# Score products of full height and operand rows at one place modulo 256, in two chained transformer blocks on one core

## The chip, the core and the metric

The kernel runs on one core of a Trainium2 chip. The metric is the device time of one execution in microseconds; the times before are 2703.43, 2702.10 and 2704.92 us, median 2703.43 us. Names of engines: PE is TensorE (PEld its weight loads), DVE is VectorE, ACT is ScalarE, POOL is GpSimd, SP is the queue that issues most DMAs.

## The reference, cut to what matters

Two blocks of two layers each run one after the other on 256 tokens of width 1024. A layer is: half a SwiGLU feed-forward (FFN), a mixer, half an FFN. Block 1 carries a second stream of 256 context tokens; block 2 has one stream. The part that the change touches is the mixer of block 1:

```python
hx = modulate(rms_norm(x), mx[3], mx[4])
qx, kx, vx, upx, ufx = split_in(hx @ w_in[layer])
s = jnp.einsum('bqkgd,bskd->bkgqs', qb, k_all) * ATTN_SCALE      # 8 query heads, 2 key heads, width 64
p = jax.nn.softmax(s, axis=-1)
yp = jnp.einsum('blgc,gcd->blgd', pool_minus_self(u_pool), pool_w_l)   # 4 groups, 64 x 64 each
```

Latent queries attend to 512 keys (latent and context), context queries, in layer 0 alone, to 256.

## The kernel before, in words

**Split products.** Operands are float32 split in a high and a low part of type fp32r (`xhi`, `xlo` for activations, `whi`, `wlo` for weights, `h` for the inner FFN activations with both parts in one tile). `mm3` (lines 245 to 249) makes every large product from three matmuls into one PSUM tile: high by high (L247), low by high and high by low (L248, L249).

**FFN.** `prod` in `ffn` runs over 8 row tiles k of the model width; for each k it issues the three products with a 128x128 stationary weight tile and the activations `xhi[:, k]`, `xlo[:, k]` as the moving operand. In the profile these are `g<-xhi,whi`, `u<-xlo,whi` and so on, 24 products per tile of 128 inner columns and matrix. They are 512 columns wide where both streams run together and 258 wide with one stream (256 tokens and two more columns). The down product (`d<-h,whi`) moves `h`, 512 or 256 wide. Mixers use the same helper: `z` has the activations stationary and moves weights, `o` (output projection) and `fp` move the activations.

**Places in SBUF.** `xhi` and `xlo` are tiles [128, 8, 514] of 4-byte elements, so `xhi[:, k]` starts 2056 bytes behind `xhi[:, k-1]`. Weights lie in 4096-byte tiles, `h` and most mixer tensors in the 4096-byte slots of the pool `blk` (`BLK` = 17 of them, `slot`). In the built program the start bytes modulo 256 are: `xhi[:, k]` 128 + 8k, `xlo[:, k]` 192 + 8k, weights 0, `blk` slots 0.

**Mixer 1** (`mixer1`, once per layer of block 1). Keys are split in `use_kv`: `kk` holds per key head four planes of 64 (line 1173 on): high, high, low, and an unused one. `turn_k` transposes them to `khh` (high over high, 128 rows) and `klo` (low, 64 rows). Queries are transposed to 128 rows, high over low. `scores` makes a head's scores from two matmuls: L1205 on all 128 rows (query high and low by key high) and L1206 on the first 64 rows (query high by key low). `attend` (line 1011 on) is software-pipelined over heads: in step i PE makes the scores of head i (`s`), transposes the probabilities of head i-2 (`tp<-c_ident,prob`, L1004) and multiplies those of head i-3 by the values (`o<-v,PT`, L1041), while DVE takes the maximum and ACT the exponential. Steps of the pooling and Fourier mixers (`pool_fft`) fill in between. Layer 0 has 16 heads of 512 keys and 16 of 256, layer 1 16 of 512. `poolw` (line 1243) multiplies two pooled groups of 64 rows by their own 64x64 weights, two plain float32 matmuls on a quarter of the array each.

The order on each engine is that of the code; no scheduler moves instructions.

Of the kernel before, what the change touches and what calls it, by code (L numbers as in the profile page):

```python
# [11 lines left out]
F32R = mybir.dt.float32r  # L12
# [7 lines left out]
P = 128  # L20
D = 1024
KT = D // P
T = 256
# [5 lines left out]
WINDOWS = (2, 4, 8, 16)  # L29

WBUF = 5
BLK = 17
AHEAD, TAIL, TEND = (3, 4, 4, 4), 0, 3
WA = (range(8), range(0, 8, 2))
FSPLIT = {False: [(0, FT)], True: [(0, FT // 2), (FT // 2, FT)]}
# [9 lines left out]
def f32v(t):  # L45
    return t.bitcast(F32)


def kp(w):
    return w.rearrange("(kt p) n -> p kt n", p=P)  # L50


class Net:
# [5 lines left out]
    def __init__(self, tc, a, es):  # L59
# [4 lines left out]
        self.wsp = pool("wsp", WBUF)  # L64
        self.blk = pool("blk", BLK)
        self.adaw = pool("adaw", 2)
# [195 lines left out]
    def setup(self):  # L262
        nc, a = self.nc, self.a
        self.x = self.const.tile([P, KT, 512], F32, name="xstate")

        self.xh = self.const.tile([P, KT, 514], F32R, name="xhi")
        self.xl = self.const.tile([P, KT, 514], F32R, name="xlo")
        self.mods = {}
        self.pairs = {l: self.const.tile([P, 2, 72], F32, name=f"mod1{l}") for l in range(2)}
        for l in range(2):  # L270
            for v in range(2):
                self.mods["1", l, v] = self.pairs[l][:, v]
            self.mods["2", l, 2] = self.const.tile([P, 72], F32, name=f"mod2{l}")
        self.ones = self.const.tile([P, 2], F32, name="ones")
        nc.vector.memset(self.ones, 1.0)
        self.mhalf = self.const.tile([P, 16], F32, name="mhalf")
        nc.vector.memset(self.mhalf, -0.5)
        self.sc01 = self.const.tile([P, KT, 2], F32, name="csilu01")
        nc.sync.dma_start(self.sc01, a["ccols"])
        nc.scalar.activation(self.sc01, self.sc01, AF.Silu)  # L280
        self.cb = {}
        self.ident = self.cload("ident", [P, P])
        self.adab = {}
        for b in "12":
            for l in range(2):
                self.adab[b, l] = self.const.tile([P, 72], F32, name=f"adab{b}{l}")
        nc.gpsimd.dma_start(self.adab["1", 0], a["ada_b1"][0])
        self.load_stream(0)
        self.cb = {}
# [816 lines left out]
    def mixer1(self, l, nx):  # L1106
        nc, a = self.nc, self.a
# [9 lines left out]
        self.fetch(gains, a["qk_gain"][l, None].to_broadcast([P, 2, 2, 64]))  # L1117
        rot = gr[:, 8:].rearrange("p (t i a) d -> p t i a d", t=2, i=2)
        khh = self.slot([P, 2, 512], "khh", F32R)
        klo = self.slot([P, 2, 512], "klo", F32R)  # L1120
        v = self.slot([P, 4, P], "v")
        zz, kk, u, qT, rq = {}, {}, {}, {}, {}
        A, B = slice(0, 32), slice(32, 64)

        def gained(dst, src, st, t, i, n):

            bc = lambda w: w.unsqueeze(1).to_broadcast([P, n, w.shape[1]])
            if st:
                nc.vector.tensor_mul(dst, src, bc(gains[:, 0, i]))
                return  # L1130
            sw = self.w2("sw")[:, :n * 64].rearrange("p (h d) -> p h d", d=64)
            nc.vector.tensor_mul(sw[:, :, A], src[:, :, B], bc(rot[:, t, 1, i, A]))
            nc.vector.tensor_mul(sw[:, :, B], src[:, :, A], bc(rot[:, t, 1, i, B]))
            nc.vector.tensor_mul(dst, src, bc(rot[:, t, 0, i]))
            nc.vector.tensor_add(dst, dst, sw)

        def squares(src, n, name):
            sq = self.w2("qks")[:, :n * 64].rearrange("p (h d) -> p h d", d=64)
            nc.scalar.activation(sq, src, AF.Square)
            m = self.sml.tile([P, n], F32, name=name + "s", tag=name + "s", bufs=2)  # L1140
            nc.vector.reduce_sum(m, sq, axis=AX.X)
            return m
# [21 lines left out]
        def use_kv(st, pss):  # L1164
            for t in range(2):
                s = pss[t][:, :P].rearrange("p (h d) -> p h d", d=64)
                nc.scalar.copy(v[:, st * 2 + t], pss[t][:, P:])
                m = squares(s, 2, "k")
                rk = self.small(2)
                nc.vector.tensor_scalar(m, m, 1.0 / 64, EPS, op0=ALU.mult, op1=ALU.add)  # L1170
                nc.gpsimd.tensor_tensor(rk, m, self.mhalf[:, :2], op=ALU.pow)
                zk = self.w1("zk")[:, :P].rearrange("p (h d) -> p h d", d=64)
                gained(zk, s, st, t, 1, 2)
                nc.vector.tensor_mul(zk, zk, rk.unsqueeze(2).to_broadcast([P, 2, 64]))
                if t == 0:
                    kt = self.slot((P, 4, 4, 64), "kk", F32R)
                kk[st, t] = kt[:, 2 * t:2 * t + 2]
                nc.scalar.copy(kk[st, t][:, :, 0], zk)
                nc.scalar.copy(kk[st, t][:, :, 1], zk)
                nc.vector.tensor_sub(kk[st, t][:, :, 2], zk, f32v(kk[st, t][:, :, 0]))  # L1180

        def turn_k(st):
            for t in range(2):
                c = slice(st * T + t * P, st * T + (t + 1) * P)
                kf = f32v(kk[st, t])
                ps = self.transposes([kf[:, g, 0:2].rearrange("p a d -> p (a d)") for g in range(2)]
                                     + [kf[:, g, 2] for g in range(2)])
                nc.scalar.copy(khh[:, :, c], ps[:, :T].rearrange("p (g c) -> p g c", g=2))
                nc.scalar.copy(klo[:64, :, c], ps[:64, T:].rearrange("p (g c) -> p g c", g=2))

        def turn_q(st):
            qT[st] = [self.slot([P, 4, T], "qT", F32R) for _ in range(2)]
# [6 lines left out]
        def batches(st):  # L1199
            k0 = 0 if st == 0 else T  # L1200
            nk = 512 - k0

            def scores(s, h, qt, nk):
                q = qT[st][h // 4][:, h % 4, qt * P:(qt + 1) * P]
                nc.tensor.matmul(s, q, khh[:, h // 4, k0:], start=True, stop=False)  # L1205
                nc.tensor.matmul(s, q[:64], klo[:64, h // 4, k0:], start=False, stop=True)  # L1206

            return [dict(heads=range(8), qt=qt, nk=nk, hd=64, scores=scores, k0=0, col=st * T,
                         scale=lambda h, qt: rq[st, qt][:, h:h + 1],
                         v=lambda c, h: v[:, k0 // P + c, 64 * (h // 4):64 * (h // 4) + 64]) for qt in range(2)]  # L1210
# [3 lines left out]
        def pool_fft(st):  # L1214

            s = slice(st * T, (st + 1) * T)
            b = {}

            def load():
                if st == 0:  # L1220
                    pw = self.slot([P, 4, 256], "pw")
                    self.fetch(pw[:, 0, :P], a["pool_w"][l])
                    self.fetch(pw[:, 1:3], kp(a["fft_w"][l]))
                    self.fetch(pw[:, 3], a["chdft"].rearrange("p a b -> p (a b)"))
                    dft = self.slot([P, 2, 512], "dft")
                    self.fetch(dft, a["dft"])
                    mats.update(pw=pw, dft=dft)
                b.update(mats)
                for i in range(2):
                    b[i] = self.slot([P, 2, 2, T], "band")  # L1230
                    self.fetch(b[i], a["band"][i])
# [10 lines left out]

            def poolw(i):
                ps = self.smps("pl")
                for g in range(2):
                    hp = slice(64 * g, 64 * g + 64)
                    nc.tensor.matmul(ps[hp, :T], b["pw"][hp, 0, i * 64:i * 64 + 64], b["yp"][hp, i],
                                     start=True, stop=True)
                return lambda: self.split_ps(self.xh[:, 4 + i, s], self.xl[:, 4 + i, s], ps[:, :T],
                                             self.pscale[:, l * 2 + i:l * 2 + i + 1])  # L1250

# [37 lines left out]
        for t in range(2):  # L1289
            nc.vector.tensor_mul(rot[:, t], gains, rope1[:, t].unsqueeze(2).to_broadcast([P, 2, 2, 64]))  # L1290
        wk = self.tok_w(win[:, :, 512:768], 256)
        use_kv(0, self.tok_mm(0, wk, 256, free=False))
        psk = self.tok_mm(T, wk, 256)
        use_kv(1, psk)
# [440 lines left out]
def _tiles(w):  # L1735

    s = w.shape[:-2]
    k, m = w.shape[-2:]
    w = w.reshape(s + (k // P, P, m // P, P))
    n = len(s)  # L1740
    return np.ascontiguousarray(w.transpose(tuple(range(n)) + (n + 2, n + 1, n, n + 3)))


def _cols(v):

    return np.ascontiguousarray(np.asarray(v).reshape(-1, P).T)
# [42 lines left out]
def _layout(i):  # L1789
    a = _constants()  # L1790
# [13 lines left out]
    g = np.stack([i["q_gain"], i["k_gain"]], 1)  # L1804
    a["qk_gain"] = np.ascontiguousarray(np.stack([g, np.roll(g, 32, -1)], 1))
    pw = i["pool_w"].reshape(2, 2, 2, 64, 64)
    a["pool_w"] = np.ascontiguousarray(pw.transpose(0, 2, 3, 1, 4)).reshape(2, P, P)
    a["pool_scale"], a["fft_w"], a["w_out"] = _cols(i["pool_scale"]), i["fft_w"], _tiles(i["w_out"])
    a["final_gain"], a["norm_g"], a["final_g"] = _cols(i["final_gain"]), _cols(i["norm_g_2"]), _cols(i["final_g_2"])
    a["pos"] = _cols(i["positions_2"])  # L1810
# [36 lines left out]
```

## Time and profile before

| what | value |
|---|---|
| median of the runs | 2703.43 us |
| the profiled execution: its own time / its span | 2702.88 us / 2700.6 us |
| PE busy | 2645.5 us (98%) in 16822 matmuls |
| PEld busy | 2366.2 us (88%) |
| DVE busy | 1889.6 us (70%) |
| ACT busy | 1120.1 us (41%) |
| POOL busy | 226.6 us (8%) |
| mean granted clock of TensorE | 0.991 of full speed |
| DMA | 489.45 MB, mean 181 GB/s |

The span is the time from the first to the last instruction on the core; 2.3 us of the execution's own time lie around it. Matmuls are pipelined: a matmul's listed duration overlaps the next one's, so what one costs in a row of them is the distance between their starts.

### The profile page before, as it was taken

To read this page: it belongs to the slowest core of one execution; us is meant where nothing else is said; L and a number is where in the kernel's file an instruction comes from. 1 tells how busy PE (TensorE), PEld (TensorE's weight loads), DVE (VectorE), ACT (ScalarE), POOL (GpSimd) and SP (SyncE) were. 2 spreads that over 40 slices of the span, in tenths; PEclk is the share of its full clock that TensorE was granted. 3 is DMA by queue.
4 is the path that set the end of the run, shared out by engine and by line. 5 is a ranking of instruction groups with operands and counts; after the bars stand their busy time and mean duration, and the time that the engine had idled before them with its cause. 6 is when DMAs were issued, how large, how long until landed. Compare 5 with 4: busy or idle time off the path is not lost.

```text
span 2700.6 us, 43302 instructions
## 1 busy us (share of the span) xinstructions
PE 2645.5 (98%) x16822; PEld 2366.2 (88%) x16822; DVE 1889.6 (70%) x3419; ACT 1120.1 (41%) x1834; POOL 226.6 (8%) x222
## 2 busy tenths in 40 slices
PE   7999999999999999999999999999989999999998
PEld 5788888688888898888879999999789999998998
DVE  7776785546777655656667777878777777767764
ACT  4422224543222242222255544445555444445543
POOL 6000022010000010000211002001010000010000
PEclk8999999999999999999999999999999999999999
DMA  5454553113454445666633677676427777653753
GB/s 222 156 188 178 185 192 118 55 34 107 169 213 172 171 149 187 237 229 221 221 125 118 235 225 237 225 239 215 136 80 240 220 246 234 221 173 127 236 182 129
DMA packets 152350, 489.45 MB, mean 181 GB/s; under 512 B 17633, under 2 KB 25857, under 8 KB 152145
## 3 DMA queue, kind: packets, MB, share of 16 engines
q1 hardware_dynamic: 149280, 479.58, 52.8%
q0 software_dynamic: 2576, 6.58, 0.7%
q8 instruction: 133, 2.18, 0.3%
q14 instruction: 73, 0.59, 0.1%
q10 hardware_dynamic: 288, 0.52, 0.1%
HBM read 485.56 MB, written 1.05 MB: 180 GB/s over the span
## 4 chain that ended last, share of the span: by engine, by line
PE 90%; DVE 4%; ACT 2%; DMA 2%; issue 1%; POOL 0%; SPq 0%; POOLq 0%; ACTq 0%; DVEq 0%
PE g L248 8%; PE u L247 8%; PE u L249 8%; PE g L247 8%; PE g L249 8%; PE u L248 8%; PE d L247 8%; PE d L248 8%; PE d L249 8%; PE z L247 1%; PE z L249 1%; PE z L248 1%; PE o L248 1%; PE o L247 1%; PE o L249 1%
## 5 line engine op out<-in xcount | busy, mean ns | idle before, releaser
L170 ACT CAST whi<-raw 128x1024 fp32r<-128x1024 f32 (+5 forms) x673 | 654.7, 981 | 564.4 <-PE u L248 165.9
L181 DVE TENSOR_TENSOR wlo<-raw,whi 128x1024 fp32r<-128x1024 f32 (+5 forms) x673 | 769.3, 1160 | 38.8 <-ACT whi L170 37.9
L352 DVE SCALAR_TENSOR_TENSOR adajunk<-adaraw,cb 128x1024 bf16<-128x1024 f32 x386 | 487.1, 1262 | 42.2 <-DMA adaraw<-ada_w 36.5
L247 PE MATMUL d<-h,whi 128*128 128x256 f32 (+1 forms) x1474 | 467.8, 317 | 0.2 <-ACT whi L170 0.2
L249 PE MATMUL d<-h,wlo 128*128 128x256 f32 (+1 forms) x1474 | 466.7, 317 | 0.4 <-DVE wlo L181 0.4
L248 PE MATMUL d<-h,whi 128*128 128x256 f32 (+1 forms) x1474 | 466.6, 317 | 0.0
L247 PE MATMUL g<-xhi,whi 128*128 128x258 f32 (+2 forms) x1440 | 462.4, 321 | 1.9 <-DVE xhi L707 1.5
L248 PE MATMUL g<-xlo,whi 128*128 128x258 f32 (+2 forms) x1440 | 462.5, 321 | 1.0 <-DVE xlo L498 0.7
L248 PE MATMUL u<-xlo,whi 128*128 128x258 f32 (+2 forms) x1440 | 461.8, 321 | 0.0
L247 PE MATMUL u<-xhi,whi 128*128 128x258 f32 (+2 forms) x1440 | 461.8, 321 | 0.0
L249 PE MATMUL u<-xhi,wlo 128*128 128x258 f32 (+2 forms) x1440 | 460.9, 320 | 0.0
L249 PE MATMUL g<-xhi,wlo 128*128 128x258 f32 (+2 forms) x1440 | 460.9, 320 | 0.0
L441 POOL TENSOR_TENSOR nacc<-nacc,nsq 128x256 f32<-128x256 f32 x114 | 131.3, 1160 | 2224.8 <-ACT nsq L439 1656.6
L249 PEld LDWEIGHTS d<-h,wlo 128*128 128x128 f32 x1474 | 281.4, 191 | 18.6 <-DVE wlo L181 0.6
L247 PEld LDWEIGHTS d<-h,whi 128*128 128x128 f32 x1474 | 281.4, 191 | 18.5 <-ACT whi L170 0.4
L248 PEld LDWEIGHTS d<-h,whi 128*128 128x128 f32 x1474 | 281.5, 191 | 18.2
L248 PEld LDWEIGHTS g<-xlo,whi 128*128 128x128 f32 x1440 | 272.4, 189 | 24.4 <-DVE xlo L722 1.2
L247 PEld LDWEIGHTS g<-xhi,whi 128*128 128x128 f32 x1440 | 271.8, 189 | 23.6 <-ACT xhi L663 1.5
L249 PEld LDWEIGHTS u<-xhi,wlo 128*128 128x128 f32 x1440 | 273.5, 190 | 20.7 <-DVE wlo L181 0.4
L248 PEld LDWEIGHTS u<-xlo,whi 128*128 128x128 f32 x1440 | 272.3, 189 | 21.9
L249 PEld LDWEIGHTS g<-xhi,wlo 128*128 128x128 f32 x1440 | 273.6, 190 | 20.2
L247 PEld LDWEIGHTS u<-xhi,whi 128*128 128x128 f32 x1440 | 271.8, 189 | 21.6
(362 smaller groups left out, 3081.2 us busy)
## 6 DMA issues: line engine op xcount, KB each, us to landing
adaraw<-ada_w SPq DMA_DIRECT2D x281, 512.0 KB, 4.5
raw<-gu SPq DMA_DIRECT2D x176, 512.0 KB, 4.5
raw<-gate SPq DMA_DIRECT2D x88, 512.0 KB, 4.4
raw<-up SPq DMA_DIRECT2D x88, 512.0 KB, 4.0
raw<-down SPq DMA_DIRECT2D x64, 448.0 KB, 4.3
raw<-dn SPq DMA_DIRECT2D x48, 384.0 KB, 5.0
raw<-down SPq DMA_DIRECT2D x32, 512.0 KB, 3.6
raw<-dn SPq DMA_DIRECT2D x48, 320.0 KB, 3.9
```

What stands on the lines that cost most here:

```text
L170: nc.scalar.copy(hi[:, :n], raw[:, :n])
L181: self.nc.vector.tensor_sub(lo, raw, hi)
L247: nc.tensor.matmul(ps, lh, rh, start=start, stop=False)
L248: nc.tensor.matmul(ps, lh, rl, start=False, stop=False)
L249: nc.tensor.matmul(ps, ll, rh, start=False, stop=stop)
L352: nc.vector.scalar_tensor_tensor(junk, raw, 1.0, self.cb[v], op0=ALU.mult, op1=ALU.mult, accum_out=dst)
L441: (eng or nc.gpsimd).tensor_tensor(box[name], box[name], sq, op=ALU.add)
```

## The change

It makes five edits, and leaves the order of work as it was.

1. `xhi` and `xlo` become [128, 8, 576], so rows lie 2304 bytes apart (9 times 256).
2. `BLK` goes from 17 to 16 slots. With the new sizes, `xhi[:, k]`, `xlo[:, k]`, all weight tiles and all `blk` slots start at 128 modulo 256 in the built program. The rows k odd of `xhi` and `xlo` start at 384 modulo 512, all the others of these at 128.
3. The fourth plane of `kk` is filled with a copy of the low part (one more ACT copy of 128x128 per 128 tokens, eight in all), `turn_k` transposes two full pairs of planes, and `kll` (low over low, 128 rows) takes the place of `klo`.
4. The second score product runs on 128 rows. It adds query low by key low, which was left out before.
5. `poolw` becomes one matmul with a block-diagonal 128x128 weight; the table `pool_w` is twice as large (128 KB instead of 64 KB per layer).

```diff
-BLK = 17
+BLK = 16
...
-        self.xh = self.const.tile([P, KT, 514], F32R, name="xhi")
-        self.xl = self.const.tile([P, KT, 514], F32R, name="xlo")
+        self.xh = self.const.tile([P, KT, 576], F32R, name="xhi")
+        self.xl = self.const.tile([P, KT, 576], F32R, name="xlo")
...
-        klo = self.slot([P, 2, 512], "klo", F32R)
+        kll = self.slot([P, 2, 512], "kll", F32R)
...
                 nc.vector.tensor_sub(kk[st, t][:, :, 2], zk, f32v(kk[st, t][:, :, 0]))
+                nc.scalar.copy(kk[st, t][:, :, 3], f32v(kk[st, t][:, :, 2]))
...
-                ps = self.transposes([kf[:, g, 0:2].rearrange("p a d -> p (a d)") for g in range(2)]
-                                     + [kf[:, g, 2] for g in range(2)])
+                ps = self.transposes([kf[:, g, i:i + 2].rearrange("p a d -> p (a d)") for i in (0, 2) for g in range(2)])
                 nc.scalar.copy(khh[:, :, c], ps[:, :T].rearrange("p (g c) -> p g c", g=2))
-                nc.scalar.copy(klo[:64, :, c], ps[:64, T:].rearrange("p (g c) -> p g c", g=2))
+                nc.scalar.copy(kll[:, :, c], ps[:, T:].rearrange("p (g c) -> p g c", g=2))
...
                 nc.tensor.matmul(s, q, khh[:, h // 4, k0:], start=True, stop=False)
-                nc.tensor.matmul(s, q[:64], klo[:64, h // 4, k0:], start=False, stop=True)
+                nc.tensor.matmul(s, q, kll[:, h // 4, k0:], start=False, stop=True)
...
-                for g in range(2):
-                    hp = slice(64 * g, 64 * g + 64)
-                    nc.tensor.matmul(ps[hp, :T], b["pw"][hp, 0, i * 64:i * 64 + 64], b["yp"][hp, i],
-                                     start=True, stop=True)
+                nc.tensor.matmul(ps[:, :T], b["pw"][:, 0, i * P:(i + 1) * P], b["yp"][:, i], start=True, stop=True)
```

## Rows read from the trace of the kernel before

**Rows 1.** The page, part 4: the chain that ended last, by engine.

```profile
PE 90%; DVE 4%; ACT 2%; DMA 2%; issue 1%; POOL 0%; SPq 0%; POOLq 0%; ACTq 0%; DVEq 0%
```

**Rows 2.** Groups of PE matmuls by line and shape: count, busy us, mean ns.

```profile
L247 PE MATMUL g<-xhi,whi 128*128 128x512 f32 x480 | 188.4, 393 | 0.4 <-ACT xhi L718 0.4
L247 PE MATMUL z<-whi,xhi 128*128 128x512 f32 x160 | 63.8, 399 | 0.0
L247 PE MATMUL g<-xhi,whi 128*128 128x258 f32 x896 | 255.3, 285 | 1.5 <-DVE xhi L707 1.5
```

**Rows 3.** Timeline of PE (start us, us, instruction): edges of four FFN stretches.

```profile
735.00 0.40 PE L247 MATMUL d<-h,whi 128*128 128x512 f32 x1
...
794.86 0.40 PE L247 MATMUL g<-xhi,whi 128*128 128x512 f32 x1
...
917.48 0.40 PE L247 MATMUL d<-h,whi 128*128 128x512 f32 x1
...
1669.43 0.37 PE L247 MATMUL g<-xhi,whi 128*128 128x258 f32 x1
1669.63 0.28 PE L248 MATMUL g<-xlo,whi 128*128 128x258 f32 x1
...
1790.74 0.28 PE L247 MATMUL d<-h,whi 128*128 128x256 f32 x1
...
1854.09 0.28 PE L247 MATMUL fp<-xhi,whi 128*128 128x258 f32 x1
```

**Rows 4.** Timeline of PE, two steps inside a 258-wide stretch.

```profile
1675.40 0.29 PE L248 MATMUL g<-xlo,whi 128*128 128x258 f32 x1
1675.53 0.28 PE L249 MATMUL g<-xhi,wlo 128*128 128x258 f32 x1
```

**Rows 5.** Timeline of PE, one head of 512 keys in layer 1.

```profile
1418.04 0.47 PE L1205 MATMUL s<-khh,qT 128*128 128x512 f32 x1
1418.44 0.50 PE L1206 MATMUL s<-klo,qT 64*128 64x512 f32 x1
1418.87 0.66 PE L1004 MATMUL tp<-c_ident,prob 128*128 128x128 f32 x4
1419.37 1.00 PE L1041 MATMUL o<-v,PT 128*128 128x64 f32 x8
```

**Rows 6.** Timeline of PE, one head of 256 keys in layer 0.

```profile
551.65 0.36 PE L1205 MATMUL s<-khh,qT 128*128 128x256 f32 x1
551.95 0.38 PE L1206 MATMUL s<-klo,qT 64*128 64x256 f32 x1
552.26 0.44 PE L1004 MATMUL tp<-c_ident,prob 128*128 128x128 f32 x2
```

**Rows 7.** Timeline of PE, a 128-row product and transposes behind it.

```profile
1393.43 0.39 PE L249 MATMUL z<-whi,xlo 128*128 128x512 f32 x1
1393.66 0.71 PE L1004 MATMUL tp<-c_ident,kk 128*128 128x128 f32 x5
```

**Rows 8.** Timeline of PE, the first two products of 512 columns after another kind.

```profile
2428.12 0.50 PE L247 MATMUL z<-whi,lop 128*128 128x512 f32 x1 [0.15 <-ACT qr L1607]
2428.45 0.40 PE L248 MATMUL z<-wlo,lop 128*128 128x512 f32 x1
```

**Rows 9.** Timeline of PE, a float32 product of 128 rows, and `poolw` with what follows.

```profile
519.17 1.03 PE L1265 MATMUL ff<-ft,pw 128*128 128x256 f32 x4
...
522.21 0.65 PE L1247 MATMUL pl<-yp,pw 64*64 64x256 f32 x4
522.79 0.49 PE L1205 MATMUL s<-khh,qT 128*128 128x512 f32 x1
```

**Rows 10.** Timeline of ACT, the first copy behind the key transposes of layer 0.

```profile
464.61 0.37 ACT L1188 CAST khh<-tp 128x256 fp32r<-128x256 f32 x1 [3.80 <-PE tp L1004]
```

**Rows 11.** Windows of the attention: us, then busy us (instructions) per engine.

```profile
537.00:559.50 22.50, 22.50 (x154) 18.39 (x153) 15.39 (x45) 14.04 (x41) 0.00 (x0) 1.00 0.08 25
1406.00:1442.50 36.50, 35.55 (x221) 26.06 (x220) 25.52 (x50) 23.85 (x50) 0.00 (x0) 1.00 0.15 45
```

More of the change, by code (lines that the diff above doesn't have):

```diff
@@ L1221, in load @@
                     pw = self.slot([P, 4, 256], "pw")
-                    self.fetch(pw[:, 0, :P], a["pool_w"][l])
+                    self.fetch(pw[:, 0], a["pool_w"][l])
                     self.fetch(pw[:, 1:3], kp(a["fft_w"][l]))
@@ L1806, in _layout @@
     pw = i["pool_w"].reshape(2, 2, 2, 64, 64)
-    a["pool_w"] = np.ascontiguousarray(pw.transpose(0, 2, 3, 1, 4)).reshape(2, P, P)
+    bd = np.zeros((2, 2, 64, 2, 2, 64), np.float32)
+    for g in range(2):
+        bd[:, g, :, :, g] = pw[:, :, g].transpose(0, 2, 1, 3)
+    a["pool_w"] = bd.reshape(2, P, 2 * P)
     a["pool_scale"], a["fft_w"], a["w_out"] = _cols(i["pool_scale"]), i["fft_w"], _tiles(i["w_out"])
```

## The prediction

> **What bounds the kernel now.** I read four views. First the page's chain: PE holds 90% of it, DVE 4%, ACT 2%, DMA 2% [rows 1]. PE is busy for 98% of the span, so time goes where PE's stream gets shorter, and a saving on another engine is worth nothing. Second the groups of PE matmuls, for how many products there are of each shape [rows 2]. Their mean durations are no price: 393 ns stands beside a product that is followed by the next one after 232 ns. Third, therefore, the timeline, for the distance from start to start. Fourth the windows of the attention, to see how much of them the other engines fill [rows 11].
>
> The reader is to see one thing in [rows 3]: the same product of the same shape has two prices. From 794.86 to 917.48 us PE makes 11 column tiles, 2 matrices, 8 rows k and 3 products each, 528 in all, that move `xhi` and `xlo` 512 wide: 122.62 us / 528 = 232.2 ns. From 735.00 to 794.86 it makes 264 that move `h` 512 wide: 59.86 / 264 = 226.7 ns. Nothing waits in either stretch. What differs is the place of the moving operand: `h` and the weights all start at 0 modulo 256, `xhi` and `xlo` at sixteen other places. In the narrow stage the difference is gone: 258 wide with `xhi`, `xlo` (1790.74 - 1669.63) / 1007 = 120.3 ns, 256 wide with `h` (1854.09 - 1790.74) / 528 = 120.0 ns.
>
> In the attention the pair of score products does not run at such steps [rows 5, 6]. The first stands 0.40 us ahead of the second, and the second, 64 rows high, 0.43 us ahead of the transposes. A 128-row product of 512 columns is followed by transposes after 0.23 us [rows 7]. So the 64-row product holds up PE's pipeline on both sides.
>
> **The change, part by part.**
>
> *Rows of xhi, xlo 2304 bytes apart.* Removed: the sixteen places. All operands of the FFN products then stand to each other as `h` and the weights do now, but for one thing: rows k odd lie 256 from the weights modulo 512, and `h` never does. I price all of them as `h`. The 512-wide products that move or hold `xhi`, `xlo`: 480 per line in three lines and two matrices is 2880 [rows 2], and 160 in three lines for `z`, where the activations are stationary, is 480. 3360 x (232.2 - 226.7) = **-18.5 us**. The bounds are 0 (no effect of place) and this value, since no row is below 226.7.
>
> The 258-wide ones: 896 in six groups, 5376. A column costs (226.7 - 120.0) / 256 = 0.417 ns by [rows 3], so 258 columns at one place take 120.0 + 0.8 = 120.8 ns. 5376 x 0.5 = **+2.7 us**. Single steps go up to 0.13 us now [rows 4]; at 0.13 throughout, 5376 x 9.7 = +52 us is the upper bound. Downwards, 120.0 gives -1.6 us. I take +2.7, since it follows from the products that already stand at one place. The remaining 256-wide products of `o`, `fp` and `g` are at 120 now and stay.
>
> Here the Trainium skill speaks against the change. Its page "TensorE: Matmul & The Clock Gate", section "Step-by-step: what each phase is for", says that TensorE reads the moving operand and the weights through two independent ports, so that loading the next weights takes nothing from the running matmul. By that rule the relative place of the two could not matter and both terms would be zero. The 232.2 against 226.7 ns at one shape speaks against it, though a place could matter for another reason than a port.
>
> *Score products of full height.* Each head of 512 keys: first to second product 0.40 us now, 0.33 as the first two 128-row products after another kind of work [rows 8]; second product to transposes 0.43 now, 0.23 as [rows 7]; the four transposes 0.66 long now, while five behind a 128-row product take 0.71, so four 0.60. Together 0.07 + 0.20 + 0.06 = 0.33 us. Each head of 256 keys: 0.30 to 0.20 (the first step of a 258-wide stretch, 1669.43 to 1669.63), 0.31 to 0.12, and 0.06 again: 0.35 us [rows 6, 3]. 32 x 0.33 + 16 x 0.35 = 16.2 us. The product of low by low columns adds no column, so nothing else comes in.
>
> *poolw as one matmul.* Six calls. Now four records (two matmuls, float32 going twice) take 0.58 us until the next score product; a float32 product of 128 rows and 256 columns takes (1.03 - 0.36) / 3 = 0.22 us per record, so two 0.44 [rows 9]. 6 x 0.14 = 0.8, and somewhat more for the stop that goes ahead of it; I take 1.0 us.
>
> What of these 17.2 us arrives? PE's saving makes each step of a head 0.33 us shorter for everyone. In the last 22.5 us of layer 0's attention DVE is busy for 15.4 and ACT for 14.0, in layer 1's 36.5 us 25.5 and 23.9 [rows 11]. After the change PE would need about 17 and 31, still above both. But the first heads of an attention wait for the softmax of the head two steps ahead, and a weight split on ACT and DVE every third step delays it. I take **-15 us**, with 7 (half lost to the softmax) and 17.2 as bounds.
>
> *Key planes.* Eight more ACT copies. Each is at most 0.37 us, the copy of twice its size [rows 10]; four per layer are 1.5 us. ACT sits idle for 3.80 us right behind them, until the key transposes, which come after the query projection. Nothing at this price, 1.5 us per layer if that cover were gone. Other edits cost nothing: the transposes of `kk` are as many and as long; the 64 KB more of `pool_w` go through POOL's queue long ahead of its use, which is in the attention. One slot fewer makes some tiles wait for another reader. In the order of the program each such reader stands well ahead of the new writer, so I put 0; no row prices it, nothing can be gained, and a loss is a step of a head at most (2.14 us, the sum of [rows 5]), if a late writer stands in an attention.
>
> **Sum.** -18.5 + 2.7 - 15 = -30.8 us. The profiled execution took 2702.88 us with a span of 2700.6; the median of the runs is 0.55 us above it. 2703.43 - 30.8 = **2672.6 us**.
>
> **The rivals.**
>
> *Half the rows.* The step repeats every 512 bytes, not every 256. Rows k odd then remain at another place than `h` ever had, and half of -15.8 stays away: -7.9 - 15, 2680.5 us. `h` and weights never differ by 256 modulo 512, so no row speaks for or against it.
>
> *Place has no part.* 232.2 against 226.7 has another cause (say, two tiles alternating), both terms are zero: 2688.4 us. The page's rule on the two ports gives the same time. Against it: nothing else differs in [rows 3], and the mean of sixteen places is what one would get from many different steps.
>
> *Softmax takes over.* PE's stream shortens, and the transposes wait for ACT's exponential or for the copy of the transposed probabilities: 7 of 15 us, 2680.6 us. For it: the busy shares of 70% that remain. Against: PE's need stays the largest.
>
> *Not the height.* PE stops because the kind of product changes from fp32r to float32, not because of 64 rows. Then the 0.43 us stay, the 0.40 fall by some 0.08 in 48 heads, 3.8 us, and 1.0 from `poolw`: 2682.8 us. Against it: [rows 7], where the kind changes too and 0.23 us pass.
>
> *The slower side: 258 columns settle badly.* At sixteen places the 258-wide steps average out; at one place all 5376 take the same step, which could be a long one, as the 0.13 us of [rows 4]. It decides from (18.5 + 15) / 5376 = 6.2 ns above 120.3. At 0.13 us the sum is -33.5 + 52, 2722 us. Against it: 256 columns at one place take 120.0 ns, and two columns more would have to cost what 24 do otherwise.
>
> **How the numbers follow.** Chances: the forecast 0.53; half the rows 0.12; place has no part 0.11; softmax takes over 0.11; not the height 0.05; the last with no part of place, 2698.6 us, 0.03; the slower side 0.05. A measurement of this kernel tells about 0.2%, 5.4 us, from no change. Faster by more: 0.92, the first five; within: 0.03; slower: 0.05. The low end takes 258 columns at 120.0 and all of the attention: -18.5 - 1.6 - 17.2, 2666 us. The high end takes in the case without a part of place, 2689 us.
>
> **What would show it.** In the changed profile: 528 products 512 wide in 119.7 us between two down stretches, against 122.6 now; steps of one value, 0.227 us, in all k, or of two values by k odd and even (half the rows). The 258-wide stretch of 1007 steps 0.5 us longer; over 6 us longer would be the slower side. Score products 0.33 and 0.23 us apart, no `issue` idle ahead of the weight load of L1206, and the attention of layer 1 near 31 us; if transposes wait for `prob` or `PT` there, the softmax took over. The prediction is wrong if 512-wide steps do not come to 0.227 us, or if PE's idle time in the attention grows by more than 3 us.

## The result and the profile after

The changed kernel takes 2675.19 us (median of four runs, 2673.82 to 2678.38) against 2702.76 us (four runs, 2701.99 to 2704.92): a ratio of 0.9898 with a 95% interval of 0.9881 to 0.9916, that is 23 to 32 us less. Forecast were 2672.6 us, in a range of 2666 to 2689. The profiled execution took 2673.82 us with a span of 2671.9, 28.7 us less than the span before.

The page, part 4, the chain by engine, to be held against [rows 1]:

```profile
PE 88%; DVE 5%; ACT 2%; DMA 2%; issue 2%; POOL 1%; SPq 0%; ACTq 0%; POOLq 0%; DVEq 0%
```

PE still carries the end, but it lost two points, and DVE, issue and POOL have one more each: PE got shorter and now waits a little more often.

Groups of PE matmuls by line and shape (count, busy us, mean ns), to be held against [rows 2]:

```profile
L247 PE MATMUL g<-xhi,whi 128*128 128x512 f32 x480 | 186.9, 389 | 0.4 <-ACT xhi L718 0.4
L247 PE MATMUL z<-whi,xhi 128*128 128x512 f32 x160 | 63.0, 394 | 0.0
L247 PE MATMUL g<-xhi,whi 128*128 128x258 f32 x896 | 254.4, 284 | 1.5 <-DVE xhi L707 1.5
```

The means moved by 1 to 5 ns and say little. The timeline of PE (start us, us, instruction) says it, at the same edges as [rows 3]:

```profile
719.18 0.39 PE L247 MATMUL d<-h,whi 128*128 128x512 f32 x1
...
779.02 0.39 PE L247 MATMUL g<-xhi,whi 128*128 128x512 f32 x1
...
898.70 0.39 PE L247 MATMUL d<-h,whi 128*128 128x512 f32 x1
...
1641.16 0.37 PE L247 MATMUL g<-xhi,whi 128*128 128x258 f32 x1
1641.36 0.28 PE L248 MATMUL g<-xlo,whi 128*128 128x258 f32 x1
...
1762.20 0.28 PE L247 MATMUL d<-h,whi 128*128 128x256 f32 x1
...
1825.56 0.28 PE L247 MATMUL fp<-xhi,whi 128*128 128x258 f32 x1
```

From 779.02 to 898.70 the same 528 products 512 wide take 119.68 us, 226.7 ns each, where [rows 3] had 122.62 and 232.2. From 1641.36 to 1762.20 the 1007 steps of 258 columns take 120.84 us, 120.0 each, and the 528 of 256 columns behind them 63.36, again 120.0.

Heads of the attention, one of 512 keys in layer 1 and one of 256 in layer 0, to be held against [rows 5] and [rows 6]:

```profile
1392.24 0.48 PE L1205 MATMUL s<-khh,qT 128*128 128x512 f32 x1
1392.56 0.39 PE L1206 MATMUL s<-kll,qT 128*128 128x512 f32 x1
1392.79 0.60 PE L1004 MATMUL tp<-c_ident,prob 128*128 128x128 f32 x4
1393.22 1.00 PE L1041 MATMUL o<-v,PT 128*128 128x64 f32 x8
1394.03 0.48 PE L1205 MATMUL s<-khh,qT 128*128 128x512 f32 x1
...
537.42 0.36 PE L1205 MATMUL s<-khh,qT 128*128 128x256 f32 x1
537.62 0.28 PE L1206 MATMUL s<-kll,qT 128*128 128x256 f32 x1
537.74 0.38 PE L1004 MATMUL tp<-c_ident,prob 128*128 128x128 f32 x2
538.10 0.66 PE L1041 MATMUL o<-v,PT 128*128 128x64 f32 x4
```

0.32 and 0.23 us stand around the second product of 512 columns, 0.20 and 0.12 around that of 256; before it was 0.40 and 0.43, 0.30 and 0.31. A head of 512 keys takes 1.79 us instead of 2.14. The head of 256 keys shows the other side: `o` starts 0.36 us behind the transposes, not 0.27, since the copy of `PT` is not there yet.

What the heads kept of this is read from windows that run from the first head of a kind to its last (us; busy us and instructions of PE, PEld, DVE, ACT, POOL; granted clock, DMA share, GB/s). Of the kernel before:

```profile
490.42:534.89 44.47, 43.53 (x250) 29.63 (x248) 24.82 (x51) 25.99 (x56) 0.00 (x0) 1.00 0.12 39
537.03:558.27 21.24, 21.24 (x146) 17.39 (x146) 14.17 (x42) 13.71 (x40) 0.00 (x0) 1.00 0.08 25
1406.70:1439.80 33.10, 32.34 (x202) 23.60 (x200) 22.89 (x45) 21.96 (x46) 0.00 (x0) 1.00 0.15 49
```

The same heads after:

```profile
482.67:522.41 39.74, 38.01 (x242) 30.70 (x240) 24.68 (x50) 26.10 (x56) 0.00 (x0) 1.00 0.15 51
524.20:543.17 18.97, 17.90 (x146) 16.29 (x146) 13.87 (x43) 12.71 (x39) 0.00 (x0) 1.00 0.08 29
1382.03:1410.96 28.93, 27.22 (x197) 24.08 (x196) 21.99 (x44) 21.96 (x46) 0.00 (x0) 1.00 0.16 55
```

Fifteen steps of each kind gave 4.73, 2.27 and 4.17 us, 11.2 in all. The heads of 256 keys gave least: PE is idle for 1.07 of their 18.97 us, and before for nothing.

The end of layer 0's attention then gives 2.1 us back. The timeline of PE there, and windows of the same place:

```profile
545.41 0.57 PE L1004 MATMUL tp<-c_ident,prob 128*128 128x128 f32 x2 [0.95 <-ACT prob L1070]
545.77 0.97 PE L1041 MATMUL o<-v,PT 128*128 128x64 f32 x4
546.51 0.77 PE L247 MATMUL o<-xhi,whi 128*128 128x512 f32 x1
```

```profile
542.00:545.60 3.60, 2.47 (x20) 1.98 (x18) 2.58 (x8) 2.48 (x9) 0.00 (x0) 1.00 0.03 5
545.60:549.00 3.40, 3.40 (x12) 2.90 (x12) 0.00 (x0) 0.71 (x3) 0.00 (x0) 0.50 0.00 0
549.00:552.40 3.40, 3.40 (x19) 2.83 (x19) 0.53 (x2) 0.00 (x0) 0.00 (x0) 1.00 0.00 0
```

The transposes wait 0.95 us for the exponential (0.40 at this place before), and right behind, the granted clock is 0.50 of full speed, the lower of its two levels (1.2 instead of 2.4 GHz), for 3.4 us, where the kernel before had 1.00. Ahead of the fall PE was busy for 2.47 of 3.60 us. In layer 1, `o` waits 0.96 us for `PT` at 1414.59, where it waited 0.16 before: 0.8 more.

So the trace's ledger is: about -20 us from the places (steps of 512 and 258 columns, over the whole kernel), -11.2 + 2.1 + 0.8 = -8.3 from the attention, together 28.3 of the 28.7 us. The opening does not close as well. The lead at the first down product is 4.14 us (173.35 before, 169.21 after), and 432 products of 512 columns explain 432 x 5.5 ns = 2.4 of it. The other 1.7 us belong to no edit, and further on 1.3 are lost again. The granted clock from 20 to 70 us was 0.83 before and 0.86 after. In the run e2 below, whose edits touch nothing up to that point, the same product starts at 170.82 us, 2.5 ahead of before: the opening moves by that much without an edit.

### The profile page after: what moved, and what is told of

Its sections match the earlier page's. It is cut to its first block, busy times and chain, and to the rows that moved or that the text cites. A ratio compares the mean times of both kernels' runs of the same rounds, so it can differ in the third digit from the quotient of the medians.

```text
span 2671.9 us, 43289 instructions
## 1 busy us (share of the span) xinstructions
PE 2611.0 (98%) x16810; PEld 2364.5 (88%) x16810; DVE 1889.8 (71%) x3419; ACT 1121.6 (42%) x1842; POOL 227.8 (9%) x222
## 4 chain that ended last, share of the span: by engine, by line
PE 88%; DVE 5%; ACT 2%; DMA 2%; issue 2%; POOL 1%; SPq 0%; ACTq 0%; POOLq 0%; DVEq 0%
PE g L248 8%; PE u L247 8%; PE u L249 8%; PE g L249 8%; PE g L247 8%; PE u L248 8%; PE d L247 8%; PE d L249 8%; PE d L248 8%; PE z L247 1%; PE z L249 1%; PE z L248 1%; PE o L248 1%; PE o L247 1%; PE o L249 1%
## 5 line engine op out<-in xcount | busy, mean ns | idle before, releaser
L247 PEld LDWEIGHTS u<-xhi,whi 128*128 128x128 f32 x1440 | 275.1, 191 | 18.5
L249 PEld LDWEIGHTS g<-xhi,wlo 128*128 128x128 f32 x1440 | 275.0, 191 | 18.5
```

Source lines behind the costliest of these rows:

```text
L247: nc.tensor.matmul(ps, lh, rh, start=start, stop=False)
L249: nc.tensor.matmul(ps, ll, rh, start=False, stop=stop)
```

## The experiments

### The two parts apart

e1 takes edits 1 and 2 alone, e2 edits 3 to 5 alone.

```diff
 e1 (on the kernel before)
-BLK = 17
+BLK = 16
-        self.xh = self.const.tile([P, KT, 514], F32R, name="xhi")
-        self.xl = self.const.tile([P, KT, 514], F32R, name="xlo")
+        self.xh = self.const.tile([P, KT, 576], F32R, name="xhi")
+        self.xl = self.const.tile([P, KT, 576], F32R, name="xlo")
 e2 (on the changed kernel): the same lines the other way round
```

> Edits 1 and 2 alone (rows 2304 bytes apart, 16 slots); scores and poolw as before. Theory (the two parts add up, the place carries most): 512-wide steps with xhi and xlo at 226.7 ns, 258-wide at 120.1, the attention as before (0.40 and 0.43 us around the second score product); opening aside, -18.5 - 1.5 = -20 us, about 2683 us. Rival (the parts help each other, since the layout also serves the attention): -15 us or less here. Rival (most of the gain of the change came from the opening and its clock, not from the place): steps at 232 ns and within 0.2% of before.

> Edits 3 to 5 alone (second score product on 128 rows, poolw as one matmul); rows 2056 bytes apart, 17 slots. Theory: the head steps are as short as in the whole change (0.33 and 0.23 us), but the softmax and the copies of PT take back half: -8 to -10 us, about 2694 us, 512-wide steps stay at 232 ns. Rival (all 17 us arrive, and what was lost in the whole change was lost to its layout): 2686 us. Rival (the attention gives nothing, the layout all): within 0.2% of before.

Measured against 2702.23 us: e1 2683.57 us, ratio 0.9927 (0.9915 to 0.9939), so -18.7; e2 2692.36 us, ratio 0.9965 (0.9952 to 0.9979), so -9.9. Together -28.5, the whole change -27.6: the parts add up within the intervals, as the theory had it. In e1 the 512-wide `xhi` and `xlo` steps are at 226.7 ns, by the edges of a stretch of 528:

```profile
785.38 0.39 PE L247 MATMUL g<-xhi,whi 128*128 128x512 f32 x1
...
905.06 0.39 PE L247 MATMUL d<-h,whi 128*128 128x512 f32 x1
```

Around the second score product stand 0.42 and 0.43 us (medians of the 32 heads of 512 keys), as before; in e2 the 512-wide steps are at 232.2 ns, and the medians 0.34 and 0.23 us. e2 ends its attention of layer 0 with the same wait as the whole change, but without the lower clock behind it (last head on, and 5.6 us further):

```profile
548.42:554.00 5.58, 4.63 (x28) 3.83 (x28) 2.11 (x6) 1.96 (x7) 0.00 (x0) 1.00 0.01 3
```

The lower clock after 545.6 us is thus not bound to that wait alone: e3 to e6 below have the wait too (0.9 to 1.0 us) and keep the full clock there, while e7 loses it as the whole change does. Of the 2.1 us, 0.55 are the longer wait, the rest, some 1.6, is the clock.

### What about the place counts

e3 leaves the rows 2304 bytes apart and shifts all weights and slots by 64 bytes, so that `xhi`, `xlo` lie 64 below the weights and `h` where they are. e4 makes the rows 2112 bytes apart, four places in turn.

```diff
 e3
+        self.pad = self.const.tile([P, 16], F32, name="pad")
 e4
-        self.xh = self.const.tile([P, KT, 576], F32R, name="xhi")
+        self.xh = self.const.tile([P, KT, 528], F32R, name="xhi")
 (xlo likewise)
```

> The whole change, with 64 unused bytes between xlo and the weights: all rows of xhi and xlo still start at 128 modulo 256, weights and h at 192. Theory A (what counts is that moving operand and weights stand at the same place): the x steps leave 226.7 ns for one other value between 226 and 239 ns, the h steps stay at 226.7. Theory B (what counts is that each product starts at the same place as the one ahead of it): x steps stay at 226.7, total within 0.2% of the change. Theory C (only full multiples of 64 bytes count): also 226.7.

> The whole change with rows 2112 bytes apart (64 modulo 256): xhi[:, k] takes the places 128, 192, 0 and 64 in turn, xlo the same, weights stay at 128. Theory A (place relative to the weights modulo 256): rows k = 0 and 4 at 226.7 ns, the other six longer, a mean between 228 and 236 ns over 24 products. Theory B (same place as the product ahead): the steps between rows change, those within a row of the same operand less, mean between 227 and 232. Theory C (multiples of 64 bytes are enough): 226.7 ns for all, total as the change.

e3 took 2693.41 us in its one run. Its timeline, the edges of a stretch of 528 products:

```profile
785.93 0.39 PE L247 MATMUL g<-xhi,whi 128*128 128x512 f32 x1
...
909.13 0.39 PE L247 MATMUL d<-h,whi 128*128 128x512 f32 x1
```

123.20 us, 233.3 ns each, the same mean in all eight rows k, while `h` stays at 226.7. That is theory A: all rows still start at one place, but not at that of the weights, and the steps are longer than the mixed ones before. B and C fall. e4 took 2690.65 us, steps between 226 and 236 ns in a pattern that repeats every four rows k, mean 231.7. That bears A out only in part. Places differ in price, but rows 0 and 4 are not at 226.7 throughout, as A had it: their three steps are about 226, 235 and 228 ns. The four distances at their prices in the table below would give a mean of 230.3. So where distances are mixed, a step depends also on the products beside it.

### The distance as a parameter

With A standing for stretches at one distance, two kernels map the step over the distance (place of the moving operand less that of the weights, modulo 256). The 113.5 ns that e5 expects were first seen in e3: its 256-wide products that move `xhi` and `xlo`, `o` among them, stand at about 114 ns, against 120 in the changed kernel. e5 has `xhi`, `xlo` at +64 and the slots, with `h`, at -64; e6 `xhi`, `xlo` at +128 and `h` at +64.

```diff
 e5 (e6: 32:546, and the pad between weights and slots)
-        self.xh = self.const.tile([P, KT, 576], F32R, name="xhi")
+        self.xh = self.const.tile([P, KT, 576], F32R, name="xhi")[:, :, 32:546]
 (xlo likewise)
+        self.blk = pool("blk", BLK)
+        self.wpad = pool("wpad", 1).tile([P, 16], F32, name="pad")
         self.wraw = pool("wraw", 4)
         self.wsp = pool("wsp", WBUF)
-        self.blk = pool("blk", BLK)
```

> The whole change with other relative places: xhi and xlo start 64 bytes above the weights modulo 256, h and the other slots 64 below. Theory A (the step is set by the distance modulo 256 and the width): h 256 wide, like the x products of that width at 64 below, falls from 120.0 to 113.5 ns (3017 products, -19 us), h 512 wide rises from 226.7 to 233.3 (1383, +9 us); x at +64 takes one constant value per width, unknown, between 226 and 240 ns at 512 columns. Rival (the gain at 256 columns was owed to short runs of o, not to the place): h 256 wide stays at 120.

> The whole change with xhi and xlo 128 bytes from the weights modulo 256, h and the other slots 64 above the weights. Theory A: one constant value per width and distance; h (256 and 512 wide) repeats what x showed at +64 in the run beside it. Rival (each tensor has its own law): h at +64 differs from x at +64 by more than 2 ns at 512 columns.

Both run once: 2665.55 and 2698.58 us. Mean steps in ns, each from stretches of 264 products or more; the tensor and run in brackets. The column for 258 counts the first step of a stretch, 0.20 us after a break; without it each value is 0.08 less.

| distance | 512 columns | 258 columns | 256 columns |
|---|---|---|---|
| 0 | 226.7 (`xhi`, `h`, after) | 120.1 (after) | 120.0 (`h`, after) |
| +64 | 228.9 (`xhi`, e5; `h`, e6) | 118.75 (e5) | 117.8 (`h`, e6) |
| -64 | 233.3 (`xhi`, e3; `h`, e5) | 120.9 (e3) | 113.4 or 117.8 (`h`, e5) |
| 128 | 232.4 (`xhi`, e6; 233.3 in one stretch) | 122.3 (e6) | not tried in long stretches |

Where two tensors stand at one distance, they agree within 0.1 ns, so the rival (each tensor its own law) falls, and `h` 256 wide left 120.0, so e5's rival falls too. One constant value per width and distance, as A had it, holds for the means only: at +64 the 512-wide steps go round in 226, 229 and 232 ns. The best distance depends on the width, and zero, to which the change brings everything, is best at 512 columns only. One thing e5 leaves open. Its stretches of 528 `d` products take one of two values:

```profile
1578.05 0.28 PE L248 MATMUL d<-h,whi 128*128 128x256 f32 x1
...
1637.91 0.28 PE L248 MATMUL g<-xhi,whi 128*128 128x258 f32 x1
...
1765.91 0.28 PE L248 MATMUL d<-h,whi 128*128 128x256 f32 x1
...
1828.10 0.28 PE L248 MATMUL fp<-xhi,whi 128*128 128x258 f32 x1
```

59.86 us is 113.4 ns a product, 62.19 is 117.8, of the same instructions at the same distance. What chooses between them was not found.

### Where the attention's missing microseconds lie

e7 takes 0.21 us per head off DVE by scaling the maximum on POOL; e8 starts the output products that fill the end of the attention one head earlier.

```diff
 e7
-                    nc.vector.tensor_scalar(m[:, 1:2], m[:, 0:1], scale, -1.0, op0=ALU.mult, op1=ALU.mult)
+                    nc.gpsimd.tensor_scalar(m[:, 1:2], m[:, 0:1], scale, -1.0, op0=ALU.mult, op1=ALU.mult)
 e8
-AHEAD, TAIL, TEND = (3, 4, 4, 4), 0, 3
+AHEAD, TAIL, TEND = (4, 4, 4, 4), -1, 3
```

> The whole change with the scaling of the maximum (128x1, 0.21 us per head on DVE) moved to POOL. Theory (in the heads of 256 keys DVE and ACT are the bound, DVE's copies of PT come late): the heads that take 1.15 us now fall toward PE's own 0.90, -1 to -2 us in layer 0, waits for DVE PT below 0.1 us. Rival (the chain of one head's softmax is the bound, not DVE's load): a further semaphore makes the chain longer, heads take 1.1 us or more and the attention gets slower by 1 to 3 us.

> The whole change with the output products that are begun in the attention's last steps started one head earlier, four instead of three in layer 0. Theory (the wait of 0.95 us for prob at the end of layer 0's attention and the clock at half speed right behind it are what the attention gave back, 2.1 us): both go, the lead at the first out product is 2 us larger in layer 0 and up to 1 us in layer 1, total -2 to -3 us against the change. Rival (PE waits for the same softmax anyway, only elsewhere): no difference beyond 0.5 us.

e7 took 2675.05 us, no gain. Its heads of 256 keys in layer 0 and its end of layer 1's attention:

```profile
524.25:542.50 18.25, 17.31 (x147) 16.37 (x146) 10.84 (x27) 12.64 (x41) 3.97 (x15) 1.00 0.08 30
```

```profile
1414.23 0.66 PE L1004 MATMUL tp<-c_ident,prob 128*128 128x128 f32 x4 [1.22 <-ACT prob L1070]
```

Each side was right in one place. The heads that took 1.15 us take 0.96, so DVE's late copy of `PT` was their limit, and the window is 0.7 us shorter. But the waits move on to ACT's copies and exponentials, and at the end of the attention, where one head's chain is all that is left, POOL's slower step (0.27 against 0.21 us) adds to it: 1.22 us of waiting in layer 1 instead of 0.96. Behind that wait the granted clock is 0.50 for 3.4 us (from 1415.78), as in e6 (from 1433.54) but not in the changed kernel, so part of what e7 lost in layer 1 is the clock's.

e8 took 2672.58 us. From the first head of layer 0 to the next FFN's first down product it needs 233.79 us (484.16 to 717.95), the whole change 236.51 (482.67 to 719.18): -2.7 us, the wait and the lower clock both gone (from the last head on):

```profile
544.63:548.57 3.94, 3.94 (x23) 3.21 (x22) 2.17 (x6) 1.65 (x6) 0.00 (x0) 1.00 0.01 4
```

In layer 1 nothing came of it (187.44 against 187.40 us over the same kind of stretch): the wait of 0.96 us is replaced by two at the split of the last heads, 1.02 together:

```profile
1422.34 0.38 PE L247 MATMUL o<-xhi,whi 128*128 128x256 f32 x1 [0.68 <-ACT xhi L255]
1423.07 0.39 PE L248 MATMUL o<-xlo,whi 128*128 128x256 f32 x1 [0.34 <-DVE xlo L256]
```

So the theory held in layer 0 and the rival in layer 1. Of the 2.7 us some 1.6 are the clock's share, and that the edit is what kept the clock up is not shown, since e2 to e6 kept it without this edit. The whole gain, 1.2 us against the profiled run of the change, is less than a measurement tells.

### Versions that use the map

e9 puts the single-stream x operands 16 columns further (distance +64 for 258 columns), moves the weights of 14 of 22 row tiles of the down product up by 64 bytes (distance -64 for `h`, 256 wide), and keeps e8's edit. e10 does the same with 32 bytes.

```diff
 e9 (e10: 8 for 16)
+Y = T + 16
-            y = slice(T, 514)
+            y = slice(Y, Y + T + 2)
 (and the places that write these columns)
+        o = 16 if shape[0] == 7 else 0
-        hi = self.wsp.tile([P, 1024], F32R, name="whi", tag="whi")
-        lo = self.wsp.tile([P, 1024], F32R, name="wlo", tag="wlo")
+        hi = self.wsp.tile([P, 1024], F32R, name="whi", tag="whi")[:, o:]
+        lo = self.wsp.tile([P, 1024], F32R, name="wlo", tag="wlo")[:, o:]
```

> The whole change, with places chosen by width: the 258-wide x operands 64 bytes above the weights modulo 256, the h products of 14 of 22 row tiles 256 wide 64 below (their weights moved up by 64), all 512-wide ones at the same place; and the output products begun one head earlier. Theory A (the step is a function of distance and width): 258-wide steps 118.75 instead of 120.1 ns, -7.2 us; 1920 d products at 113.4 to 117.8 instead of 120.0, -4 to -13 us; 512-wide steps stay at 226.7; the tail -1 to -2.6 us. Together 2653 to 2663 us. Rival (the price is set over the whole stage, and mixing distances costs what it gives): d products at 120 or above, 2665 us or more.

> As the run beside it, with 32 bytes in the place of 64. Theory A with a smooth dependence on the distance: 258-wide steps between 118.75 and 120.1 ns, d at 32 below between 115 and 120. Rival (the dependence is not smooth, single distances stand out): outside these.

e9: 2659.06 us against 2700.39, ratio 0.9849 (0.9836 to 0.9863). The 258-wide steps are 118.75 ns, the 512-wide stay at 226.7, `d` means 118.6, as the eight row tiles left at distance zero keep 120.0 and the others take 117.8. Time and steps lie within theory A, and the rival falls. e10 took 2669.54 us: at 32 bytes the 258-wide steps go round in 120, 120, 124 and 116 ns, mean 120.1, no better than at zero, and `d` means 118.8, with some 118.1 for the 14 row tiles. Both lie within the bounds set for a smooth dependence, the first at its very edge, so one run at 32 bytes leaves it open whether 64 stands out.

e11 gives all 22 row tiles the distance -64 and leaves the weights alone; for that the slots become 4352 bytes (17 times 256) and one fewer. The places of x and the end of the attention are as in e9.

```diff
-BLK = 16
+BLK = 15
 (and Y, AHEAD and TAIL as in e9)
...
+        o = 48 if name == "h" and self.late else 0
+        t = self.blk.tile([P, 1088], dt, name=name, tag="blk")[:, o:o + n]
```

> As e9, but the weights stay where they were and all 22 row tiles of h lie 64 bytes below them when 256 wide: the slots become 4352 bytes, 15 of them. Theory A: all 3017 d products of that width at 113.4 or 117.8 ns (both values stood in e5) instead of 118.6: -2.4 to -15.7 us against e9, 2643 to 2657 us. Rival (one slot fewer is one too few): PE waits at slots, 2662 us or more.

2646.52 us (2644.49 to 2647.87) against 2703.18: a ratio of 0.9791 (0.9778 to 0.9805). Its timeline, the edges of a down stretch of 528:

```profile
1563.95 0.28 PE L253 MATMUL d<-h,whi 128*128 128x256 f32 x1
...
1623.79 0.28 PE L253 MATMUL g<-xhi,whi 128*128 128x258 f32 x1
```

59.84 us, 113.3 ns each, and here every stretch of 528 takes that value; of the last FFN's six stretches of 66, one (from 2603.67) stands at 117.8. PE's stretches start no later than in e9, so the rival falls. At 56.7 us below the kernel before this is twice the gain of the change. The second half, 29 us, comes from places chosen by width (5376 x 1.3 ns and 3036 x 6.7 ns are 27 us) and, for the small rest, from e8's edit.

## Why the prediction was right

**Places, 512 wide: -18.5 us.** Right to the nanosecond: 232.2 to 226.7 in all rows k, and e1's 18.7 us agree with the sum. *Half the rows* fell (rows k odd are as fast as even ones), and so did *place has no part*. e3 shows the cause by itself: nothing but the distance of 64 bytes differs from the change, and the step goes from 226.7 to 233.3 ns. The Trainium skill's page "TensorE: Matmul & The Clock Gate", section "Step-by-step: what each phase is for", weighed in the prediction, has the moving operand and the weights come through two independent ports, so that loading weights takes nothing from the running matmul. The trace does not agree with it as a rule on time: at one shape the step is 226.7 or 233.3 ns by the distance of the two operands alone. By what mechanism the distance acts, no run here shows.

**258 columns: +2.7 us.** Mis-sized. The step that failed is "258 columns at one place take 120.0+0.8": the price of a column, 0.417 ns, was taken from 256 against 512 columns, as if steps grew evenly. 258 columns take the same 120.0 ns as 256, and the 5376 products became (121.31 - 121.04) us / 1008 x 5376 = 1.4 us cheaper, from [rows 3] and the rows above: near the bound of -1.6. The slower side, a bad step for 258 columns, did not come at distance zero; at 128 (e6, 122.3 ns) it would have been 2 ns, a third of what it needed.

**Head steps: 17.2 us.** Right: 0.35 us per head of 512 keys (forecast 0.33), and 0.35 per head of 256 (1.25 to 0.90 us) where PE waits for nothing. *Not the height* fell: the kind of product still changes behind the second score product, and only 0.23 us pass.

**Of these, 15 arrive.** Too many: about 8 did (-11.2 in the heads, +2.9 at the two ends, of which 1.6 are the lower clock). The step that failed is "After the change PE would need about 17 and 31, still above both". It compares sums over windows. In the heads of 256 keys DVE and ACT are each busy for some 13 of 19 us, but what they do for a head is a chain, maximum, scaling, exponential, transposes and copy, each waiting for the one ahead, and three operations of 0.69 us each (two divisions by the sums, one split) stand on DVE between the heads; e7 shows that a lighter DVE gains 0.7 us there and hands the rest of the wait to the next in the chain. This is what *softmax takes over* described, with its 7 of 15 us: with 258 columns at the measured -1.4 that rival comes to 2676.5 us, nearer to the measured 2675.19 than the forecast. And a sign that the prediction named against itself came: PE's idle time in the attention grew by over 3 us, from 1.7 us in the three windows and 0.6 at the two ends behind them to 4.5 and 1.9. It was the attention's term that was wrong by it; the total stayed in its range. That the clock would fall there was in no case of the prediction.

**Sum.** -18.5 + 2.7 - 15 = -30.8 forecast; measured -27.6. The two sizes that were off have opposite signs, -4.1 at 258 columns and +7 in the attention: that the sum came so near to the forecast is in part luck. The 2.14 us that the prediction calls the sum of [rows 5] is right, but as the distance from one head's start to the next (1418.04 to 1420.18 us), which those rows do not show.

**Key planes, `poolw`, the slot.** PE waits no longer than before for what comes of `kk`, and not at all for `pool_w`. The ACT copies used part of their cover: ACT's idle time ahead of the first `khh` copy of layer 0 fell from 3.80 [rows 10] to 1.86 us. e11 runs with one slot fewer still. `poolw` was not tried alone, but its six calls now take 0.24 to 0.35 us each up to the next score product, where they took 0.58: 1.6 us, and not 1.0, inside the sums of the attention.

## What to carry to other kernels

When the same product has two prices in one trace, compare the start addresses of its two operands: here their distance modulo 256 moves a step by up to 6%, and the best distance depends on the width, so measure it per width before choosing a layout (three kernels gave the map, and it was worth nearly as much as the whole change again). Price a removed stall on PE by steps, but where two engines pass one head's result back and forth, bound what arrives by the chain of one head, not by busy sums; and look at the end of the pipeline, where the waits go first.

## What the runs showed of the hardware that was not expected

- The step of a matmul is not even in its width: 256 and 258 columns both take 120.0 ns at distance zero.
- At 256 columns a distance of -64 bytes is faster than none (113.3 against 120.0 ns), at 512 it is slower (233.3 against 226.7).
- Steps take a few products to settle after a break: the last FFN's down products, in stretches of 66 behind transposes, start in the changed kernel with 201, 118 and 117 ns and stand at 120 from the fourth on; in e11 one such stretch (from 2595.95) goes 201, 120, 116, 116, 114, 114 and then 113. In e5 a stretch settles at one of two values, 113.3 or 117.8.
- The granted clock fell to its lower level for 3.4 us at the end of an attention, behind a stretch in which PE was busy for 2.47 of 3.60 us; in e2 to e6, with the same wait at the same place of the program, it did not fall. The kernel before has such stretches too, elsewhere (from 987.65 and from 1349.47 us, 0.50 each).
